# A two-layer decoder trunk on one core: modulation steps paced by matmul work, a packed rotary key, and a merge that takes its last head pair late

## The chip, the cores and the metric

The kernel runs on one core of a Trainium2 chip. The metric is the device time of one execution in microseconds (us). TensorE multiplies matrices into PSUM banks; VectorE, ScalarE and GpSimd do elementwise work; SyncE (SP) issues every DMA, in the order of its queue. Each engine runs its own instructions in order and waits on semaphores for what others produce.

## The reference

Two layers work on x, 1024 tokens by 1024 channels, in float32. Each layer is modulated by a vector `c`: shift, scale and gate vectors for two sub-layers come from one product with `w_ada`. The first sub-layer has one combined input projection, a stick-breaking attention, a latent attention (MLA) with rotary keys, and a gated merge. The second is an MLP with a squared ReLU.

```
mod = c_act @ w_ada[l] + b_ada[l]        # 6 vectors of 1024
shift1, scale1, gate1, shift2, scale2, gate2 = split(mod, 6)
h = rms_norm(x, g_mix_norm[l]) * (1 + scale1) + shift1
q_sb, k_sb, v_sb, q_lat, kv_lat, k_rope, gate_sb, gate_mla = split(h @ w_in[l])
o_sb  = stick_breaking(q_sb, k_sb, v_sb) @ w_sb_out[l]
q, kv = rms_norm(q_lat) @ w_q_up[l], rms_norm(kv_lat) @ w_kv_up[l]
k_pe  = rope(k_rope)                     # 32 channels, shared by 8 heads
o_mla = softmax_attention(q with rope, kv, k_pe) @ w_mla_out[l]
merged = sigmoid(gate_sb) * o_sb + sigmoid(gate_mla) * o_mla
x = x + gate1 * (merged @ w_mix_out[l])
h = rms_norm(x, g_mlp_norm[l]) * (1 + scale2) + shift2
x = x + gate2 * (square(relu(h @ w_up[l])) @ w_down[l])
```

After both layers, one more RMS norm gives the output.

## The kernel before

**Precision and tiles.** Activations lie transposed, channels on 128 partitions and tokens in two halves of 512. To keep float32 accuracy each operand is split in a high and a low part, and a product is three matmuls per 128 channels (`mm3_k`): high by high, high by low, low by high. A 1024-channel product of 128 outputs and one half is 24 matmuls of 512 columns into one bank.

**The planner.** The kernel is not emitted as it is written. `Plan.record` collects every operation with its tiles, `Plan.schedule` places them on five modelled engines by estimated costs, and `emit` writes them out in that order. TensorE's operations are due in the order in which they are recorded, and of those that are ready the earliest is taken; the due times of all others follow backwards from the TensorE work that needs them. Tiles of a class (`Cls`) take its slots strictly in the order of recording, and a slot that two classes share goes to the later class once the earlier has placed all its tiles. So where in the program a step is recorded decides how urgent it is.

**The modulation.** `modulation(l, parts)` is a generator. It makes a 1024-long vector in four pieces of 256: four steps per piece, each with one load of 256 KB of `w_ada` into a buffer of class `AD` and two products on VectorE (`mac`) into an accumulator of class `A`. `finish` then splits the accumulator (ScalarE copy, GpSimd subtraction, two more `A` tiles) and sums it over the partitions with four small matmuls into a `tp` bank. In the mixing sub-layer it makes parts 2 to 5 of the layer's own vectors, 64 steps. In the MLP it makes parts 0 and 1 of the next layer, 32 steps. `AD` has two buffers and `A` three. `finish` goes one step further at each load of the next piece, so a piece's first matmul is recorded two steps after its last load.

**The mixing sub-layer** (`layer`). First the latents (five jobs of `linear`, names `lraw`, `lh`, `ll`), then their norm (`lat_norm`), then a list of jobs: the rotary key (`kr_job`: 32 of the 128 weight columns in use), the first pair's queries, keys and values, and four gates. Here each half of a job takes two modulation steps. Then comes the loop over four head pairs with the products from the latents (weights in `qp` and `parts`), the rotary queries for every second pair, and a gate. Here each half takes one step, or two for a gate. Results are split and stored to DRAM by `keep_split` and `rope`, whose tiles come from `ltmp`: class `lt` in the first part, class `lt2`, four slots, in the loop.

**Attention and merge.** Attention works through pairs of heads, with other jobs filled in between. Its results go to DRAM by way of class `O`. Afterwards `outputs("mla")` loads them back through the six buffers of class `T`, splits them into `H` tiles, and `w_mla_out` is applied by `linear`, eight jobs of two halves, with `merge` as evacuation.

Of the kernel before, what the change touches and what calls it, by code (L numbers as in the profile page):

```python
# [20 lines left out]
P = 128  # L21
# [20 lines left out]
ON_ACT = (0, 2, 4, 6)  # L42

CHUNKS = (2, 2, 4)


def bc(ap):
# [128 lines left out]
class Plan:  # L176
    def __init__(self, nc):
        self.nc = nc
        self.ops, self.tiles = [], []
        self.slot_users = {}  # L180
        self.early = 0.0
        self.after = set()
        for n in ENG:
            setattr(self, n, Engine(self, n))

# [5 lines left out]
    def record(self, engine, method, a, k):  # L191
        a = tuple(View(x) if isinstance(x, PTile) else x for x in a)
        k = {n: View(x) if isinstance(x, PTile) else x for n, x in k.items()}
        outs, ins = [], []
        for i, x in enumerate(a):
            if isinstance(x, View):
                (outs if i == 0 and "out" not in k else ins).append(x)
        for n, x in k.items():
            if isinstance(x, View):
                (outs if n in ("out", "accum_out") else ins).append(x)  # L200
        op = Op()
        op.i = len(self.ops)
        op.eng = ENG[engine]
        if method == "dma_start":
            op.eng = "DMA"
        op.early = self.early
        op.func = str(k.get("func", "")).split(".")[-1]
        op.dur = cost(op.eng, method, a, k, outs, ins)
        op.succs, op.news, op.tiles = [], [], []
        nc = self.nc  # L210

        def fn():
            r = lambda x: x.resolve() if isinstance(x, View) else x
            getattr(getattr(nc, engine), method)(*[r(x) for x in a], **{n: r(x) for n, x in k.items()})  # L214
        op.fn = fn
        preds = set(self.after)
        for v in outs + ins:
            if getattr(v.tile.cls, "psum", False):
                v.box = [(0, n) for n in v.tile.shape]
        for v in ins:  # L220
            t = v.tile
            for box, o in t.writes:
                if overlap(box, v.box):
                    preds.add(o)
        for v in outs:
            t = v.tile
            for box, o in t.writes:
                if overlap(box, v.box):
                    preds.add(o)
            for box, o in t.reads:  # L230
                if overlap(box, v.box):
                    preds.add(o)
        for v in ins:
            v.tile.reads.append((v.box, op.i))
        for v in outs:
            t = v.tile
            t.writes = [(b, o) for b, o in t.writes if not covers(v.box, b)] + [(v.box, op.i)]
            t.reads = [(b, o) for b, o in t.reads if not covers(v.box, b) or o == op.i]
        preds.discard(op.i)
        op.preds = preds  # L240
        seen = set()
        for v in outs + ins:
            t = v.tile
            if id(t) in seen:
                continue
            seen.add(id(t))
            op.tiles.append(t)
            if not t.ops and t.cls.slots:
                op.news.append(t)
                t.cls.tiles.append(t)  # L250
            t.ops.append(op.i)
        self.ops.append(op)
# [237 lines left out]
class Trunk:  # L490
    def __init__(self, ctx, tc, I, out):
# [15 lines left out]
        slots = [f"s{i}" for i in range(46)]  # L507
        self.hs, self.ws, self.V = slots[:16], slots[16:22], slots[22:]
        self.T = self.cls("T", [f"t{i}" for i in range(6)])
        self.AD = self.cls("AD", ["ad0", "ad1"])  # L510
        self.A = self.cls("A", ["a0", "a1", "a2"])
        self.O = self.cls("O", ["o0", "o1"])
        self.ST = self.cls("ST", ["st0", "st1", "st2", "st3"])
        self.B = {}
        self.make_ps = maker(ps)
# [16 lines left out]

    def weight_slots(self, *more):
        self.W = {"raw": self.cls("raw", self.ws[:2]), "parts": self.cls("parts", self.ws[2:] + [*more])}

    def vcls(self, name, *idx):
        return self.cls(name, [self.V[i] for i in idx])
# [135 lines left out]
    def modulation(self, l, parts):  # L673
# [22 lines left out]
        for m in parts:  # L696
            for c0 in range(0, D, 256):
                acc = self.tile(self.A, [P, 256])
                for k0 in range(0, KT, 2):
                    w = self.tile(self.AD, [P, 2, 256])  # L700
                    v = I["w_ada"][l, k0 * P : (k0 + 2) * P, m * D + c0 : m * D + c0 + 256]
                    nc.sync.dma_start(out=w, in_=cols(v))
                    next(before, None)
                    for k in range(2):
                        self.mac(acc, w[:, k, :], k0 + k)
                    yield
# [421 lines left out]
    def layer(self, l, xT, ssq, before):  # L1128
# [3 lines left out]

        self.new_h()
        hh, hl = self.hh, self.hl

        qd, kd, vd, md, gd, od = {}, {}, {}, {}, {}, {}

# [50 lines left out]
        kr = 2176  # L1188

        def kr_w():  # L1190
            raw = self.tile(self.W["raw"], [P, KT, P])
            nc.gpsimd.memset(raw, 0.0)
            for i in range(2):
                nc.sync.dma_start(out=raw[:, :, 64 * i : 64 * i + 16], in_=win(kr + 16 * i, 16))
            return self.split_w(raw, KT)

        def lat_norm(b, tiles, width, g):
            for hf, sl in enumerate(HALVES):
# [20 lines left out]
        c_ll = self.vcls("ll", *range(5))  # L1219
        latl = [self.full(c_ll, F32R) for i in range(5)]  # L1220
        c_lt = self.vcls("lt", 15, 16, 17, 23, *range(5, 8))
        x_d = [self.dt([P, S]) for k in range(KT)]
        for k in range(KT):
            nc.sync.dma_start(out=x_d[k], in_=xT[k])
        if l == 0:
            for (_, evac, _), ps in zip(jobs, banks):
                evac(ps, HALVES[0])
            for (_, evac, _), w in zip(jobs, ws):
                ps = self.bank("pp")
                self.mm3(ps, w, hh, hl, HALVES[1], KT)  # L1230
                evac(ps, HALVES[1])
        self.weight_slots()
        if l > 0:
            for _ in self.linear(jobs[:4], hh, hl, KT, halves_first=True):
                pass
        for _ in self.linear(jobs[4:], hh, hl, KT):
            pass
        if l == 0:
            self.rope_tables(ltmp)
        cos, sin = self.full(c_cs), self.full(c_cs)  # L1240
# [1 line left out]
        nc.sync.dma_start(out=sin, in_=self.sin_d)  # L1242
        lat_norm(0, range(0, 3), QR, "g_q_lat")
        lat_norm(1, range(3, 5), KVR, "g_kv_lat")
        kr_job = (kr_w, lambda ps, sl: rope(ps, sl, 16, kpe_d), P)
        ada = self.modulation(l, [2, 3, 4, 5])
        for _ in self.linear([kr_job] + qkv(0) + [gate(m) for m in range(4)], hh, hl, KT):
            next(ada, None)
            next(ada, None)

        c_qp, c_lt = self.vcls("qp", 16, 17, *range(18, 24)), self.vcls("lt2", 15, 5, 6, 7)

        def by_heads(src, k0, k1, c0, nh, width, groups, cls):

# [24 lines left out]
        for p in range(4):  # L1279
# [2 lines left out]
                wq = q_parts(p // 2)  # L1282
            q_w = part(wq, p % 2 * P)
            for _ in self.linear([(q_w, self.keep_split(mq[p], ltmp), P)], lath, latl, 3):
                next(ada, None)
            wkv = kv_parts(p)
            k_w, v_w = part(wkv, 0), part(wkv, P)
            kv_jobs = [(k_w, self.keep_split(mk[p], ltmp), P), (v_w, self.keep(mv[p]), P)]
            for _ in self.linear(kv_jobs, lath[3:], latl[3:], 2):
                next(ada, None)  # L1290
            if p % 2 == 0:
                g = p // 2
                qr_d[g] = self.two()
# [1 line left out]
                for sl in HALVES:  # L1295
                    ps = self.bank("pp")
                    self.mm3(ps, w, lath, latl, sl, 3)
                    rope(ps, sl, 64, qr_d[g])
                    next(ada, None)
            for _ in self.linear([gate(4 + p)], hh, hl, KT):  # L1300
                next(ada, None)
                next(ada, None)
        for _ in ada:
            pass

        self.attention_banks()

        def sb_head(p, e):
            def load():
# [103 lines left out]
            return evac  # L1413

        oh, ol = outputs("mla")
        for _ in self.linear([(out_w(I["w_mla_out"], m), merge(m), P) for m in range(KT)], oh, ol, 4):
            pass
        for k in range(KT):
            nc.sync.dma_start(out=xT[k], in_=x_d[k])
# [17 lines left out]
        for _ in range(KT):  # L1437
            next(steps)

        V, hs = self.V, self.hs  # L1440
        c_f, c_b1 = self.cls("hf", hs[:8]), self.cls("b1", hs[8:])
        c_b12, c_b22 = self.cls("b12", V[8:12]), self.cls("b22", V[12:16])
        c_t13, c_t24 = self.cls("t13", V[16:]), self.cls("t24", V[:8])
# [18 lines left out]

        NP = DFF // P // 2
        hid = [self.dt([P, 8, HALF]) for m in range(NP)]
        ada = self.modulation(l + 1, range(2)) if l + 1 < DEPTH else iter(())

        def hidden(f):
# [258 lines left out]
```

## Time and profile before

| | |
|---|---|
| median of 3 runs | 3226.88 us (3220.65 to 3230.88) |
| the profiled execution's own time | 3225.95 us |
| its span, first to last instruction | 3224.2 us |
| TensorE (PE) matmul busy | 3081.9 us, 96% |
| VectorE (DVE) busy | 2219.3 us, 69% |
| ScalarE (ACT) busy | 1537.2 us, 48% |
| GpSimd (POOL) busy | 1177.9 us, 37% |
| moved by DMA | 527.20 MB, mean 164 GB/s |

PE is the matmul row, and weight loads (PEld) overlap it. Matmul records overlap in a pipeline, so the time of one is read from start to start. PEclk is the granted clock as a share of full speed. DMA share is the mean busy share of the core's 16 DMA engines. Nearly all operations are recorded by one helper line, L214, so operations are told apart by their tiles, written out<-in.

### The profile page before, as it was taken

To read this page: it belongs to the slowest core of one execution; us is meant where nothing else is said; L and a number is where in the kernel's file an instruction comes from. 1 tells how busy PE (TensorE), PEld (TensorE's weight loads), DVE (VectorE), ACT (ScalarE), POOL (GpSimd) and SP (SyncE) were. 2 spreads that over 40 slices of the span, in tenths; PEclk is the share of its full clock that TensorE was granted. 3 is DMA by queue.
4 is the path that set the end of the run, shared out by engine and by line. 5 is a ranking of instruction groups with operands and counts; after the bars stand their busy time and mean duration, and the time that the engine had idled before them with its cause. 6 is when DMAs were issued, how large, how long until landed. Compare 5 with 4: busy or idle time off the path is not lost. (4 is left out here: it accounts for less than half of the span.)

```text
span 3224.2 us, 42816 instructions
## 1 busy us (share of the span) xinstructions
PE 3081.9 (96%) x14823; PEld 2500.9 (78%) x14823; DVE 2219.3 (69%) x3238; ACT 1537.2 (48%) x2633; POOL 1177.9 (37%) x942
## 2 busy tenths in 40 slices
PE   5998999999999999999999989999999999999998
PEld 4876777888777787877777767878887777888786
DVE  7476656668667676698867546656766777559886
ACT  4432556667344444434443235666754444444343
POOL 3222434211233654345432324441113345534442
PEclk9999999999999999999999999999999999999999
DMA  6458645445843654955144774454466445476522
GB/s 223 152 175 260 189 119 130 106 110 156 288 129 112 204 185 167 286 158 173 66 133 128 248 223 126 114 148 107 115 212 200 134 138 179 157 227 212 182 85 86
DMA packets 439868, 527.20 MB, mean 164 GB/s; under 512 B 32338, under 2 KB 310500, under 8 KB 439652
## 3 DMA queue, kind: packets, MB, share of 16 engines
q1 hardware_dynamic: 439652, 524.48, 53.1%
q8 instruction: 117, 1.92, 0.3%
q14 instruction: 99, 0.81, 0.1%
HBM read 362.36 MB, written 162.00 MB: 163 GB/s over the span
## 5 line engine op out<-in xcount | busy, mean ns | idle before, releaser
L214 PE MATMUL pp<-H,parts 128*128 128x512 f32 x4032 | 1062.5, 407 | 9.2 <-ACT H L214 8.1
L214 PEld LDWEIGHTS pp<-H,parts 128*128 128x128 f32 x4032 | 739.8, 191 | 158.9 <-ACT H L214 9.3
L214 PE MATMUL pp<-bo,ws 128*128 128x512 f32 x2688 | 628.4, 395 | 14.0 <-POOL ws L214 7.5
L214 PEld LDWEIGHTS pp<-bo,ws 128*128 128x128 f32 x2688 | 503.2, 188 | 136.8 <-POOL ws L214 10.1
L214 POOL TENSOR_TENSOR parts<-raw,parts 128x1024 fp32r<-128x1024 f32 (+2 forms) x158 | 321.1, 2033 | 707.4 <-ACT parts L214 663.2
L214 POOL TENSOR_TENSOR ws<-wr,ws 128x1024 fp32r<-128x1024 f32 x112 | 299.8, 2684 | 370.0 <-ACT ws L214 344.7
L214 PE MATMUL pp<-t,pw 128*128 128x512 f32 x1344 | 324.3, 400 | 12.4 <-ACT pw L214 7.6
L214 PEld LDWEIGHTS pp<-t,pw 128*128 128x128 f32 x1344 | 255.2, 191 | 75.2 <-ACT pw L214 9.4
L214 ACT CAST parts<-raw 128x1024 fp32r<-128x1024 f32 (+2 forms) x158 | 141.6, 897 | 258.5 <-PE pp L214 231.9
L214 DVE TENSOR_TENSOR wtl<-tp,wth 128x512 fp32r<-128x512 f32 (+3 forms) x384 | 207.5, 551 | 67.8 <-ACT wth L214 65.6
L214 PE MATMUL pp<-b,pw 128*128 128x512 f32 x1008 | 243.1, 398 | 0.4 <-DVE u L214 0.3
L214 DVE SCALAR_TENSOR_TENSOR x<-pp,const,x 128x512 f32<-128x512 f32 x256 | 180.6, 742 | 89.0 <-PE pp L214 88.9
L214 DVE TENSOR_TENSOR_SCAN F<-F,sc 128x128 f32<-128x128 f32 (+7 forms) x128 | 171.7, 1349 | 94.2 <-ACT F L214 72.5
L214 DVE SCALAR_TENSOR_TENSOR A<-AD,const,A 128x256 f32<-128x256 f32 x280 | 182.9, 653 | 75.9 <-DMA AD<-in_w_ada 70.8
L214 DVE TENSOR_TENSOR bo<-T,bo 128x512 fp32r<-128x512 f32 x224 | 221.6, 1038 | 17.7 <-ACT bo L214 17.2
L214 ACT CAST wth<-tp 128x512 fp32r<-128x512 f32 (+3 forms) x384 | 180.8, 481 | 92.8 <-PE tp L214 87.3
L214 POOL TENSOR_TENSOR pw<-T,pw 128x512 fp32r<-128x512 f32 x112 | 161.1, 1457 | 173.9 <-ACT pw L214 166.3
L214 PEld LDWEIGHTS pp<-b,pw 128*128 128x128 f32 x1008 | 189.2, 189 | 45.3 <-DVE u L214 0.8
L214 POOL TENSOR_TENSOR W<-W,F 128x127 f32<-128x127 f32 (+7 forms) x128 | 153.5, 1205 | 188.1 <-ACT W L214 103.3
L214 ACT CAST bo<-T 128x512 fp32r<-128x512 f32 x224 | 135.1, 620 | 175.2 <-DMA T<-dram 133.9
L214 ACT CAST ws<-wr 128x1024 fp32r<-128x1024 f32 x112 | 116.8, 1049 | 157.0 <-PE pp L214 138.6
L214 PE MATMUL tp<-const,W 128*128 128x128 f32 x1152 | 183.1, 273 | 5.0 <-DVE wtl L214 4.4
(153 smaller groups left out, 4581.1 us busy)
## 6 DMA issues: line engine op xcount, KB each, us to landing
T<-dram SPq DMA_DIRECT2D x352, 256.0 KB
dram<-T SPq DMA_DIRECT2D x208, 256.0 KB
dram<-u SPq DMA_DIRECT2D x92, 512.0 KB
AD<-in_w_ada SPq DMA_DIRECT2D x160, 256.0 KB
raw<-in_w_in SPq DMA_DIRECT2D x68, 512.0 KB
wr<-in_w_down SPq DMA_DIRECT2D x64, 512.0 KB
pr<-in_w_up SPq DMA_DIRECT2D x56, 512.0 KB
sq<-dram SPq DMA_DIRECT2D x96, 256.0 KB
```

The costliest lines, as they stand in the source:

```text
L214: getattr(getattr(nc, engine), method)(*[r(x) for x in a], **{n: r(x) for n, x in k.items()})
```

## The change

- `Plan` sums the modelled cost of all TensorE operations in `pe`. From the latents on, `pace` takes as many modulation steps as `pe` has grown since then in units of 3.0 us (`ADA_STEP`). The fixed counts per job are gone.
- `finish` is advanced once at the first load of the next piece (the split), and its matmuls are recorded after that piece's last load.
- In the mixing sub-layer `AD` has a third buffer, the slot `V[7]`. That slot was `lt2`'s fourth. `A` has five slots; two are those of `O`, which is now made anew for the attention.
- The rotary key packs high and low weights into the 128 columns, in blocks of 32. Each half takes 16 matmuls, and the blocks are added after a copy out of the bank.
- The first two jobs of the MLA output projection take three head pairs for both halves in four banks first, and then the last pair for all four.

```
+ADA_STEP = 3.0
 Plan.__init__:
+        self.pe = 0.0
 Plan.record:
+        if op.eng == "PE":
+            self.pe += op.dur
 Trunk.__init__:
-        self.AD = self.cls("AD", ["ad0", "ad1"])
-        self.A = self.cls("A", ["a0", "a1", "a2"])
-        self.O = self.cls("O", ["o0", "o1"])
+    def mod_slots(self, *more):
+        self.AD = self.cls("AD", ["ad0", "ad1", *more])
+        self.A = self.cls("A", ["a0", "a1", "a2", "o0", "o1"])
 modulation:
                     nc.sync.dma_start(out=w, in_=cols(v))
-                    next(before, None)
+                    if k0 == 0:
+                        next(before, None)
 layer:
         def kr_w():
-            raw = self.tile(self.W["raw"], [P, KT, P])
+            raw = self.tile(self.W["raw"], [P, KT, 2, 32])
             nc.gpsimd.memset(raw, 0.0)
             for i in range(2):
-                nc.sync.dma_start(out=raw[:, :, 64 * i : 64 * i + 16], in_=win(kr + 16 * i, 16))
-            return self.split_w(raw, KT)
+                nc.sync.dma_start(out=raw[:, :, i, :16], in_=win(kr + 16 * i, 16))
+            w = self.tile(self.W["parts"], [P, KT, 2, 2, 32], F32R)
+            nc.scalar.copy(out=w[:, :, :, 0], in_=raw)
+            nc.gpsimd.tensor_sub(w[:, :, :, 1], raw, bc(w[:, :, :, 0]))
+            return w
+
+        def kr_products():
+            w = kr_w()
+            for sl in HALVES:
+                ps = self.bank("pp")
+                for k in range(KT):
+                    a = w[:, k].rearrange("p a b c -> p (a b c)")
+                    nc.tensor.matmul(ps, a, hh[k][:, sl], start=k == 0, stop=False)
+                    nc.tensor.matmul(ps, a, hl[k][:, sl], start=False, stop=k == KT - 1)
+                s, u = ltmp(), ltmp()
+                nc.scalar.copy(out=s, in_=ps)
+                for r in (0, 64):
+                    nc.scalar.copy(out=u[r : r + 32], in_=ps[r + 32 : r + 64])
+                    nc.vector.tensor_add(s[r : r + 32], s[r : r + 32], u[r : r + 32])
+                rope(s, sl, 16, kpe_d)
+                yield
...
+        self.mod_slots(V[7])
+        ada = self.modulation(l, [2, 3, 4, 5])
+        begin, taken = nc.pe, 0
+        def pace():
+            nonlocal taken
+            while nc.pe - begin > taken * ADA_STEP:
+                next(ada, None)
+                taken += 1
...
         (latents: pace() after every half)
-        kr_job = (kr_w, lambda ps, sl: rope(ps, sl, 16, kpe_d), P)
-        ada = self.modulation(l, [2, 3, 4, 5])
-        for _ in self.linear([kr_job] + qkv(0) + [gate(m) for m in range(4)], hh, hl, KT):
-            next(ada, None)
-            next(ada, None)
-        c_qp, c_lt = self.vcls("qp", 16, 17, *range(18, 24)), self.vcls("lt2", 15, 5, 6, 7)
+        first = self.linear(qkv(0) + [gate(m) for m in range(4)], hh, hl, KT)
+        for _ in self.chain([kr_products(), first]):
+            pace()
+        c_qp, c_lt = self.vcls("qp", 16, 17, *range(18, 24)), self.vcls("lt2", 15, 5, 6)
...
         (loop over the pairs: pace() in place of each next(ada, None))
         self.attention_banks()
+        self.O = self.cls("O", ["o0", "o1"])
...
-        for _ in self.linear([(out_w(I["w_mla_out"], m), merge(m), P) for m in range(KT)], oh, ol, 4):
+        first = [(out_w(I["w_mla_out"], m)(), merge(m)) for m in range(2)]
+        first = [(w, evac, sl, self.bank("pp")) for w, evac in first for sl in HALVES]
+        for w, evac, sl, ps in first:
+            for k in range(3):
+                self.mm3_k(ps, w, oh, ol, sl, k, 4)
+        for w, evac, sl, ps in first:
+            self.mm3_k(ps, w, oh, ol, sl, 3, 4)
+            evac(ps, sl)
+        for _ in self.linear([(out_w(I["w_mla_out"], m), merge(m), P) for m in range(2, KT)], oh, ol, 4):
             pass
...
         (MLP)
+        self.mod_slots()
         ada = self.modulation(l + 1, range(2)) if l + 1 < DEPTH else iter(())
```

## Rows read from the trace of the kernel before

**Rows 1.** Waits of TensorE, whole trace: who waited for whom, total us, times, longest.
```profile
PE tp L214 <- ACT A L214: 30.9, 20, 3.1
```

**Rows 2.** Waits of TensorE from 120 to 340 us.
```profile
PE tp L214 <- ACT A L214: 19.3, 10, 3.1
```

**Rows 3.** Waits of TensorE from 1660 to 1930 us.
```profile
PE tp L214 <- ACT A L214: 11.6, 10, 2.6
```

**Rows 4.** Waits of TensorE from 900 to 1660 us.
```profile
PE tp L214 <- POOL A L214: 4.5, 1, 4.5
```

**Rows 5.** Slices of layer 0: us, PE busy (matmuls), granted clock, DMA share, GB/s.
```profile
190.00:200.00 10.00, 7.10 (x27) 0.83 0.48 142
...
270.00:280.00 10.00, 8.62 (x34) 0.83 0.88 283
280.00:320.00 40.00, 37.19 (x164) 1.00 0.88 275
...
330.00:340.00 10.00, 6.83 (x29) 0.91 0.96 249
```

**Rows 6.** Layer 1: PE, PEld, DVE, ACT, POOL busy, clock, DMA share, GB/s.
```profile
1860.00:1870.00 10.00, 9.85 (x38) 8.07 (x39) 4.68 (x10) 3.20 (x8) 1.10 (x2) 0.83 0.93 306
...
1890.00:1900.00 10.00, 7.36 (x30) 5.66 (x29) 5.67 (x11) 2.65 (x5) 2.75 (x7) 0.90 0.73 220
```

**Rows 7.** Tile AD, 150 to 350 us: ns min/median/max, first to last; VectorE idle until.
```profile
L214 DVE SCALAR_TENSOR_TENSOR A<-AD,const,A x98: 460/485/2586, 183.6 to 347.9; 128x256 f32<-128x256 f32 x98
L214 SPq DMA_DIRECT2D AD<-in_w_ada x54: 367/383/1002, 184.1 to 343.8; - x54
...
  DMA AD<-in_w_ada: 38.9, 25
```

**Rows 8.** Tile AD, 1725 to 1905 us.
```profile
L214 SPq DMA_DIRECT2D AD<-in_w_ada x54: 367/383/902, 1739.3 to 1891.4; - x54
```

**Rows 9.** TensorE in order of time, layer 1's latents: start, us, operation, count.
```profile
1654.79 53.37 PE L214 MATMUL pp<-H,parts 128*128 128x512 f32 x229
```

**Rows 10.** Layer 0, 160 to 200 us; columns as in rows 6.
```profile
160.00:180.00 20.00, 20.00 (x90) 16.26 (x89) 19.89 (x33) 14.68 (x23) 4.04 (x2) 1.00 0.25 76
180.00:200.00 20.00, 17.10 (x72) 13.60 (x71) 19.45 (x30) 6.88 (x15) 10.22 (x10) 0.91 0.48 144
```

**Rows 11.** VectorE in order of time: the last piece of the latent norm.
```profile
190.26 0.68 DVE L214 TENSOR_TENSOR ll<-lraw,lh 128x512 fp32r<-128x512 f32 x1
```

**Rows 12.** TensorE in order of time: the first matmul from the normed latents.
```profile
217.28 0.39 PE L214 MATMUL pp<-lh,qp 128*128 128x512 f32 x1
```

**Rows 13.** ScalarE, first head pair of layer 0; in brackets the idle time before.
```profile
219.91 0.59 ACT L214 CAST lt<-pp 128x512 fp32r<-128x512 f32 x1 [1.11 <-PE pp L214]
221.99 0.59 ACT L214 CAST lt<-pp 128x512 fp32r<-128x512 f32 x1 [1.49 <-PE pp L214]
225.84 0.59 ACT L214 CAST lt<-pp 128x512 fp32r<-128x512 f32 x1 [3.26 <-DVE A L214]
...
232.28 0.59 ACT L214 CAST lt<-pp 128x512 fp32r<-128x512 f32 x1 [1.70 <-DMA dram<-lt]
```

**Rows 14.** TensorE where layer 0's MLA output projection begins.
```profile
838.91 0.49 PE L214 MATMUL pp<-H,parts 128*128 128x512 f32 x1 [2.73 <-ACT H L214]
```

**Rows 15.** Tile O, 780 to 860 us: the attention's last stores.
```profile
L214 SPq DMA_DIRECT2D dram<-O x6: 451/452/452, 783.7 to 810.6; - x6
```

**Rows 16.** ScalarE in order of time: the last operand of that projection.
```profile
845.55 0.62 ACT L214 CAST H<-T 128x512 fp32r<-128x512 f32 x1 [1.63 <-DMA T<-dram]
```

**Rows 17.** VectorE, first head pair of layer 0.
```profile
221.51 0.68 DVE L214 TENSOR_TENSOR lt<-pp,lt 128x512 fp32r<-128x512 f32 x1
...
226.72 0.69 DVE L214 TENSOR_TENSOR lt<-pp,lt 128x512 fp32r<-128x512 f32 x1 [0.94 <-DMA dram<-lt]
```

**Rows 18.** SP's queue, first head pair of layer 0: start, us, DMA, count.
```profile
223.63 2.55 SPq L214 DMA_DIRECT2D AD<-in_w_ada  x2
226.22 2.46 SPq L214 DMA_DIRECT2D dram<-lt  x4
```

More of the change, by code (lines that the diff above doesn't have):

```diff
@@ L1134, in layer @@
         hh, hl = self.hh, self.hl
+        V = self.V
         qd, kd, vd, md, gd, od = {}, {}, {}, {}, {}, {}
@@ L1234, in layer @@
             for _ in self.linear(jobs[:4], hh, hl, KT, halves_first=True):
-                pass
+                pace()
         for _ in self.linear(jobs[4:], hh, hl, KT):
-            pass
+            pace()
         if l == 0:
@@ L1244, in layer @@
         lat_norm(1, range(3, 5), KVR, "g_kv_lat")
-        kr_job = (kr_w, lambda ps, sl: rope(ps, sl, 16, kpe_d), P)
-        ada = self.modulation(l, [2, 3, 4, 5])
-        for _ in self.linear([kr_job] + qkv(0) + [gate(m) for m in range(4)], hh, hl, KT):
-            next(ada, None)
-            next(ada, None)
-        c_qp, c_lt = self.vcls("qp", 16, 17, *range(18, 24)), self.vcls("lt2", 15, 5, 6, 7)
+        first = self.linear(qkv(0) + [gate(m) for m in range(4)], hh, hl, KT)
+        for _ in self.chain([kr_products(), first]):
+            pace()
+        c_qp, c_lt = self.vcls("qp", 16, 17, *range(18, 24)), self.vcls("lt2", 15, 5, 6)
         def by_heads(src, k0, k1, c0, nh, width, groups, cls):
@@ L1284, in layer @@
             for _ in self.linear([(q_w, self.keep_split(mq[p], ltmp), P)], lath, latl, 3):
-                next(ada, None)
+                pace()
             wkv = kv_parts(p)
@@ L1289, in layer @@
             for _ in self.linear(kv_jobs, lath[3:], latl[3:], 2):
-                next(ada, None)
+                pace()
             if p % 2 == 0:
@@ L1298, in layer @@
                     rope(ps, sl, 64, qr_d[g])
-                    next(ada, None)
+                    pace()
             for _ in self.linear([gate(4 + p)], hh, hl, KT):
-                next(ada, None)
-                next(ada, None)
+                pace()
         for _ in ada:
@@ L1438, in layer @@
             next(steps)
-        V, hs = self.V, self.hs
+        hs = self.hs
         c_f, c_b1 = self.cls("hf", hs[:8]), self.cls("b1", hs[8:])
```

## The prediction

> **What bounds the kernel now.** I read four views in this order: where TensorE waited in the whole trace, then in the two stretches where a layer's modulation vectors are made, then those stretches slice by slice, then the loads and the vector steps that feed them. TensorE is busy for 96% of the span, so only what it waits for, and the matmuls it need not do, can give time back. Its waits for the modulation's split (`tp <- ACT A`) come to 30.9 us [rows 1], 19.3 of them in layer 0 [rows 2] and 11.6 in layer 1 [rows 3]; one more wait for the same vectors stands in the MLP, 4.5 us [rows 4]. Behind such stalls the granted clock falls from its upper level (2.4 GHz) to the lower (1.2) for a part of a slice. A granted clock of 0.83 over 10 us is 1.7 us of work not done, so layer 0's slices lose (0.17 + 0.17 + 0.09) x 10 = 4.3 us [rows 5] and layer 1's (0.17 + 0.10) x 10 = 2.7 us [rows 6]: 7.0 us that hang on the same stalls.
>
> Why do the splits come late? In layer 0, 54 modulation loads are issued between 184.1 and 343.8 us, one in 2.96 us; in layer 1, 54 in 152.1 us, one in 2.82 [rows 7, 8]. A 512-column matmul takes 53.37/229 = 0.233 us [rows 9]. The code asks for two steps (one load each) per 24 matmuls up to the heads' loop, one in 2.80 us, and in that loop for 12 steps per 108 matmuls, one in 2.10 us. The chain of load, two products and buffer release gives one in 2.8 to 3.0. It falls behind, VectorE sits 38.9 us waiting for the loads [rows 7], and TensorE, which meets a piece's first matmul two steps after its last load, waits.
>
> **Pace, lag, slots.** A step per 3.0 us of the planner's matmul cost (0.2163 us each by its formula) is one per 13.9 matmuls, 3.23 us on the chip. That is slower than the 2.82 to 2.96 that the old chain reached with two buffers and a short lead. The matmuls of a piece now come four steps later, and five A slots instead of three let two pieces wait ready: the lead grows from about two steps to more than six, some 20 us, against a longest stall of 3.1 us. So nearly all of the 30.9 us should go. I leave 3 us for the last piece of each layer, which still drains without lag: -28 (bounds -31 and -15, the last if half of the stalls stay), with it 0.9 of the clock loss, -6 (bounds -7 and 0). The lag holds for the MLP's modulation too: -4 of the 4.5 us (0 to -4.5).
>
> What pays for the earlier steps: their loads now go through SP's queue and the DMA engines from the latents on, where the engines are 0.25 to 0.48 busy (160 to 200 us, [rows 10]) against 0.88 in the later slices [rows 5]. The extra slots also let up to four more loads (1 MB, 3.8 us at the 275 GB/s of [rows 5]) slip into layer 0's start. On VectorE the stretch from 160 to 200 is full: 39.3 of 40 us [rows 10]. It gets some six more steps, each two products of 0.485 us [rows 7], so 6 us, and from the rotary key below 2.7 us. What is late then is the latent norm, whose last pieces end near 191 us [rows 11], and whose first reader on TensorE starts at 217.3 [rows 12]: 26 us of cover, some 20 after TensorE's own gain by then. So I put 2 us on all this (0 to 8).
>
> **Rotary key.** 24 matmuls per half become 16; two halves, two layers: 32 x 0.233 = 7.5 us off TensorE, in a stretch where it has no gap [rows 10]. The new evacuation adds, per half, three ScalarE copies (nearest: 0.59 us from a bank [rows 13]) and two 32-partition additions on VectorE (nearest: 0.68, [rows 11]), 2.7 us of VectorE a layer, counted above; ScalarE is busy 14.7 and 6.9 of 20 us there [rows 10]. The bank comes free after one copy rather than after VectorE's rotary products. -7.5, 0 if another engine took over there.
>
> **Merge.** TensorE waits 2.73 us when the attention output projection begins [rows 14], once a layer. The change puts 36 matmuls ahead of the last head pair's. But the last attention store is issued at 810.6 us [rows 15], 28 us before that stall, and the last cast of an operand (845.55, [rows 16]) comes 7 us after it without a wait of its own. What is late are the first operands, which queue for the six T buffers behind the stores of the other branch; that the change doesn't touch. Behind it, the third weight tile waits until two of four banks are done: its ScalarE and VectorE work was covered by 15 matmuls and is now covered by six. -1 (bounds -5.5, both stalls gone, and +3).
>
> **The buffer that is taken away.** The third load buffer was the fourth slot of `lt2`, which holds the split results of queries and keys until their stores land, and the rotary working tiles. This has a price. In the first pair the splits go in at 219.91, 221.51 and 221.99; with four slots, the fifth, sixth and seventh start at 225.84, 226.72 and 232.28 [rows 13, 17], the last two on a store. So slots are held 5.9, 5.2 and 10.3 us. Part of the longest is the SP queue: its store is issued at 226.22, behind two modulation loads that took 2.55 us [rows 18]. Two pairs of heads hold 20 stored tiles and 4 short ones (about 3 us each), while TensorE needs 198 x 0.233 = 46 us for them. With holding time L, four slots need (20 L + 12)/4 us, three need (20 L + 12)/3: 44 us at L = 6, 51 at L = 7. Four slots are never short at these values; three are at the edge. The third load buffer takes the 2.55 us off SP, so I take L = 6, where only bursts cost: 2 us for each two pairs, four times: +8. Below, 0 if L falls to 5 (37 us). Above, at L = 7.4 it is 53 us, 7 over, +28.
>
> The Trainium skill's page "DMA: Bandwidth & Descriptors" (section Anatomy of one DMA) gives about 2.0 us fixed plus bytes/436 GB/s for a transfer. By that a 256 KB store lands in an estimated 2.6 us, a slot is free after some 4 us, and the sum would be 8 us lower. The trace disagrees for this stretch: the store issued at 226.22 freed its slot 6.1 us later [rows 13, 18].
>
> **Sum.** -28 - 6 - 4 - 7.5 - 1 + 8 + 2 = -36.5 us. The profiled execution took 3225.95 us (1.75 outside its span), 0.93 under the median of the runs. 3225.95 - 36.5 = 3189.5; against the median, 3190 us.
>
> **Rivals.**
> *A: the smaller slot pool takes over (slower).* Evacuations stand in line for stores, banks fill, TensorE waits for `pp`. For: slots were held up to 10.3 us. Against: TensorE had no such wait in either stretch [rows 2, 3], and the loads that block SP thin out. Without the slot term the sum is -44.5. At L = 9 two pairs need 64 us, 18 over, four times 72: 3225.95 - 44.5 + 72 = 3253. It turns slower by more than 0.3% from L = 8.4 on (60 us, 14 over, 56). Chance 0.08.
> *B: the loop stays bound by transfers.* DMA engines at 0.88 and 275 GB/s [rows 5] have little left, so loads stay late at any pace and two thirds of the stalls remain: -10 - 2 for stalls and clock, -7.5, and nothing else of note: 3226 - 19.5 = 3206. Against: by the pace 512/13.9 = 37 of a layer's 64 loads lie ahead of the heads' loop, where before it was 10 + 33.2/2.96 = 21 (ten ahead of 184.1 us, the rest at the old rate to 217.3). Chance 0.10.
> *C: VectorE is the new bound before the heads' loop.* The products and the rotary key's additions stand in a stretch that is full already. Some products take 2.586 us instead of 0.485 [rows 7]. If ten of the sixteen added operations lost those 2.1 us, VectorE would be 9 + 21 us later, 10 past its cover, in each layer: 3189.5 + 20 = 3210. It begins from five on. The skill's page "SBUF — State Buffer" (section SBUF: two separate sides) has it that VectorE operations with two SBUF inputs and GpSimd operations that read SBUF exclude each other for a whole instruction; the long products fit that rule, and it speaks against moving work there. Chance 0.04.
> *D: the planner doesn't do what the code says.* It orders by its own costs, so the pace only moves due times, and every later instruction order may shift with it: the gain is the 7.5 us of matmuls plus or minus the listed waits elsewhere: 3219. Chance 0.06.
>
> **Chances and range.** The forecast has 0.72 (its own range 3168 to 3212), A 0.08, B 0.10, C 0.04, D 0.06. Best ends together (-31 - 7 - 4.5 - 7.5 - 5.5) give 3170; upwards the range goes on to B, C and most of D. 80%: 3166 to 3221. A measurement tells about 0.3% (9.7 us) from no change. Faster by more: the forecast, B, most of C, a part of D: 0.84. Within: 0.09. Slower: A, 0.07.
>
> **What would show it.** Right: the `tp <- ACT A` waits fall from 30.9 to under 5 us; slices at 0.83 clock vanish from both stretches; modulation loads begin in the latents and end before the attention; the rotary key has 32 matmuls a layer; the merge's stall stays near 2.7 us. The slot term shows as new `pp` waits on `lt` in the heads' loop, 8 us in all, and longer idle of ScalarE and VectorE until `dram <- lt`. Wrong: more than 28 us of such waits (A), modulation waits above 15 us with full DMA slices (B), a wait of the first `lh` matmuls (C), or losses in the attention or the MLP, which I cost at nothing.

## The result, and the profile after

The changed kernel takes 3213.28 us in the median (20 executions, 3206.58 to 3226.48) against 3231.17 before (20, 3220.65 to 3238.16): ratio 0.9948, 95% interval 0.9939 to 0.9957. It is 17 us faster by the ratio, as forecast in sign, and less than half of the 36.5 us in size. The profile was taken on the slowest of the 20 executions (3226.48 us). So a second profile of the same kernel stands beside it below, from an execution of 3209.42 us; its six executions gave a ratio of 0.9938 (0.992 to 0.9956).

TensorE's waits in the changed kernel, whole trace (`ws` are the weights of the MLP's down projection, `u` the MLP's combinations, `vT` the attention's values, `lt` the split results of queries and keys):

```profile
PE pp L218 <- POOL ws L218: 12.6, 10, 2.4
PE pp L218 <- ACT u L218: 11.2, 3, 9.2
...
PE tp L218 <- DMA vT<-dram: 10.1, 7, 2.2
PE tp L218 <- ACT A L218: 8.2, 7, 2.1
...
PE pp L218 <- DVE T L218: 5.9, 3, 3.4
PE pp L218 <- DVE lt L218: 5.6, 3, 2.7
...
PE pp L218 <- ACT lt L218: 1.2, 1, 1.2
```

The same in its second profile:

```profile
PE pp L218 <- ACT u L218: 11.0, 3, 9.2
...
PE pp L218 <- POOL ws L218: 10.1, 8, 2.4
PE tp L218 <- DMA vT<-dram: 8.3, 7, 1.9
PE tp L218 <- ACT A L218: 7.3, 4, 2.1
```

The kernel before, in the rows of the same view that answer to these:

```profile
PE pp L214 <- POOL ws L214: 7.5, 6, 1.7
...
PE tp L214 <- DMA vT<-dram: 5.4, 4, 2.5
...
PE pp L214 <- ACT u L214: 4.8, 3, 2.7
```

What was to go has gone: the waits for the modulation's split fell from 30.9 us [rows 1] to 8.2 and 7.3 us (under 5 was forecast), all of it in layer 0, and the one in the MLP [rows 4] is gone. But all rows of this view together come to 132.7 us before and 136.0 and 124.8 after. `ACT u` and `ws` in the MLP and `vT` in the attention have grown, `lt` in the heads' loop is new. The first profile is of an execution as long as the profiled one of before (3225.95 us), so its sum can't show a gain. The second is 16.5 us shorter, with 7.9 us less of waits and 8.1 us less of matmuls. The mean granted clock is 0.988 before and 0.986 and 0.988 after: the clock gave nothing.

Where the second profile gains and loses shows in the same work: first and last matmul of each layer's stick-breaking scores (`sc<-sq`), and of layer 0's down projection (`bo,ws`). Before:

```profile
L214 PE MATMUL sc<-sq,sq x192: 274/390/793, 331.1 to 582.6; 128*128 128x512 f32 x96, 128*128 128x256 f32 x64, 128*128 128x384 f32 x32
L214 PE MATMUL pp<-bo,ws x1344: 387/394/505, 1321.2 to 1645.7; 128*128 128x512 f32 x192
L214 PE MATMUL sc<-sq,sq x192: 275/390/502, 1913.5 to 2163.4; 128*128 128x512 f32 x96, 128*128 128x256 f32 x64, 128*128 128x384 f32 x32
```

The changed kernel's second profile:

```profile
L218 PE MATMUL sc<-sq,sq x192: 274/391/776, 320.6 to 573.8; 128*128 128x512 f32 x96, 128*128 128x256 f32 x64, 128*128 128x384 f32 x32
L218 PE MATMUL pp<-bo,ws x1344: 387/395/793, 1312.9 to 1643.8; 128*128 128x512 f32 x192
L218 PE MATMUL sc<-sq,sq x192: 275/389/506, 1898.3 to 2147.8; 128*128 128x512 f32 x96, 128*128 128x256 f32 x64, 128*128 128x384 f32 x32
```

Up to layer 0's attention it gains 10.5 us, and from the end of the down projection to layer 1's attention 13.3. In the down projection it loses 6.4, from layer 0's attention to that projection 2.2, and behind layer 1's start of attention it gains 1.4: 16.6 us in all (spans of 3224.2 and 3207.6).

### The profile page after: what moved, and what is told of

It reads as the page before. It is cut to its first block, busy times and chain, and to the rows that moved or that the text cites. A ratio compares the mean times of both kernels' runs of the same rounds, so it can differ in the third digit from the quotient of the medians.

```text
span 3224.7 us, 42818 instructions
## 1 busy us (share of the span) xinstructions
PE 3079.3 (95%) x14791; PEld 2497.0 (77%) x14791; DVE 2242.2 (70%) x3246; ACT 1542.2 (48%) x2647; POOL 1184.0 (37%) x942
## 4 chain that ended last, share of the span: by engine, by line
PE 60%; DVE 16%; DMA 12%; issue 5%; ACT 5%; POOL 1%; SPq 1%; DVEq 0%; ACTq 0%; POOLq 0%
PE pp L218 47%; PE tp L218 8%; PE sc L218 4%; DVE A L218 3%; DMA T<-dram 3%; DVE bo L218 2%; DMA dram<-T 2%; DVE T L218 2%; DMA AD<-in_w_ada 2%; DVE x L218 1%; DVE wr L218 1%; DMA dram<-lt 1%; ACT F L218 1%; ACT W L218 1%; DVE F L218 1%
## 5 line engine op out<-in xcount | busy, mean ns | idle before, releaser
L218 PE MATMUL pp<-bo,ws 128*128 128x512 f32 x2688 | 635.3, 397 | 19.0 <-POOL ws L218 12.6
L218 DVE TENSOR_TENSOR bo<-T,bo 128x512 fp32r<-128x512 f32 x224 | 218.5, 1022 | 17.1 <-ACT bo L218 16.6
L218 DVE SCALAR_TENSOR_TENSOR A<-AD,const,A 128x256 f32<-128x256 f32 x280 | 196.6, 702 | 45.6 <-DMA AD<-in_w_ada 40.4
L218 PE MATMUL pp<-merged,parts 128*128 128x512 f32 x768 | 182.0, 398 | 5.8 <-POOL parts L218 2.9
```

## The experiments

All ratios are against the kernel before on the same chip; TensorE times are from one profile each. "The changed kernel" is the one under study.

### The parts alone

**The changed kernel again.** No edit.

> The changed kernel, unaltered, once more with a profile. Its first profile (3226.48 us) was the slowest of its 20 executions, so it says little of where the median's gain sits. If the loss in the attention and the MLP seen there (up to the first layer's attention it is 8.5 us ahead, at the end 0) belongs to the order of the instructions, this profile shows the same new waits (ws, u, vT) at the same places. If it belongs to that execution, they are gone and the lead is kept to the end: about 3213 us, ratio 0.995.

3209.42 us, ratio 0.9938 (0.992 to 0.9956). It reaches layer 0's attention at 320.6 us (331.1 before) and keeps more of the lead, but the waits for `u`, `ws` and `vT` stand at the same places. They belong to the order of the instructions; how long each is belongs to the execution. Not all of it is the modulation's: with the rotary key alone (below) `vT` is 8.4 us and `ws` 8.5.

**The modulation alone.** The diff without `kr_products` and without the merge's new order:

```
-        for _ in self.chain([kr_products(), first]):
+        kr_job = (kr_w, lambda ps, sl: rope(ps, sl, 16, kpe_d), P)
+        for _ in self.linear([kr_job] + qkv(0) + [gate(m) for m in range(4)], hh, hl, KT):
...
-            for k in range(3):
-                self.mm3_k(ps, w, oh, ol, sl, k, 4)
...
+        for _ in self.linear([(out_w(I["w_mla_out"], m), merge(m), P) for m in range(KT)], oh, ol, 4):
```

> The modulation part alone (pace, lag, third load buffer, five A slots); rotary key and merge as before. By the prediction's terms -28 - 6 - 4 + 8 + 2 = -28 us, ratio 0.991. If the modulation gives less than predicted because other waits take its place in the same stretch, about -10 to -15 us (0.996). If the planner's new order elsewhere takes it back, anything from -10 to +5 us with the modulation waits gone all the same.

Ratio 0.9963 (0.9947 to 0.998): 12 us faster, between 6 and 17. The split's waits fall to 4.2 us, yet all waits together only from 132.7 to 129.8: `ACT u` is 10.4, `vT` 10.0, `ws` 9.6, `lt` 8.8. That profile is of an execution of 3226.42 us, no shorter than the one of before, so its sum of waits doesn't show where the 12 us of the median lie.

**The rotary key alone.** `kr_products` in place of `kr_job`; the slots, the lag and the steps as before:

```
-                    if k0 == 0:
-                        next(before, None)
+                    next(before, None)
...
-                pace()
+                next(ada, None)
```

> The rotary key in 32 matmuls alone, all else as before. By the count of matmuls -7.5 us, ratio 0.9977. If that stretch isn't bound by TensorE (VectorE full, modulation loads late), the time saved there is spent waiting for the modulation: 0 to -2 us. If the new order elsewhere counts for more than the part, it lies outside -10 to 0.

Ratio 0.9978 (0.9966 to 0.9989), 7 us faster (4 to 11), which agrees with the price of 32 matmuls.

**The merge alone.** The kernel before with the changed kernel's lines ahead of `self.linear` in the merge (`for k in range(3)`, then the fourth pair and `evac`) and nothing else of the diff.

> The merge that takes the last pair late, alone. Predicted -1 us (between -5.5 and +3), with the wait of about 2.7 us in each layer still there. If the last pair was what came late, -4 to -5.5 us and that wait gone. Outside this range: the planner's order elsewhere.

Ratio 1.0005 (0.9992 to 1.0018). From 828 to 1000 us the waits for `H` and weights get shorter by as much as the next product's wait for `merged` is new:

```profile
PE pp L214 <- DVE merged L214: 2.7, 1, 2.7
PE pp L214 <- ACT H L214: 1.8, 1, 1.8
PE pp L214 <- POOL parts L214: 1.2, 3, 0.6
```

Before, in the same stretch:

```profile
PE pp L214 <- POOL parts L214: 2.8, 2, 1.6
PE pp L214 <- ACT H L214: 2.7, 1, 2.7
```

The three parts add up: -12 - 7 + 1.6 = -17 us. What is missing is missing in the modulation, as far as single ratios tell (see the control).

### Layer 0: can the steps be early?

**Sums in another bank.** `sums` is "pp" in the mixing sub-layer and "tp" in the MLP.

```
-            ps = self.bank("tp")
+            ps = self.bank(sums)
```

> The changed kernel, but the modulation's sums in the mixing sub-layer go to a bank of pp instead of tp. Theory: in layer 0 the modulation stands still from 130 to 187 us (no product on VectorE), since its tp bank is recorded behind the four tp banks of the latent norm and banks are given in the order of recording; the steps that were to be early are made up later at more than the chain can do, and four waits of 7.3 us with their clock loss remain. Then here the products go on through 130 to 187 us, the waits for ACT A in layer 0 fall from 7.3 to under 3 us, and the time falls by 5 to 12 us against the changed kernel (3198 to 3206 us, ratio to before near 0.991). Rival: the loads or VectorE (busy 9.8 of 10 us from 160 to 190) hold it back there in any case: same time within 4 us, products still missing, or the latent norm late instead.

Ratio 0.9982 (0.9971 to 0.9994), slower than the changed kernel. The view is VectorE's time in the modulation's products by stretches (us, busy, count, clock, DMA share, GB/s). The changed kernel's second profile:

```profile
90.00:130.00 40.00, 10.30 (x16) 1.00 0.52 170
130.00:180.00 50.00, 0.00 (x0) 1.00 0.50 159
180.00:310.00 130.00, 56.45 (x96) 0.96 0.77 251
```

With the sums in pp:

```profile
130.00:180.00 50.00, 10.15 (x22) 0.90 0.67 208
```

The hold-up is real and the bank order is its cause: the products now run through. But the first matmul from the normed latents comes at 224.8 us (213.1 in the changed kernel's second profile), and layer 0's attention at 332.0 (320.6). Up to there TensorE now waits for banks of pp, above all until VectorE has added a sum (`const`) and so freed its bank. With the sums in pp, from 120 to 226 us:

```profile
PE pp L218 <- DVE const L218: 3.9, 2, 3.6
PE pp L218 <- ACT T L218: 1.4, 1, 1.4
```

All waits of that view come to 6.9 us; in the second profile up to its first matmul from the normed latents they are 2.0. All engines from 160 to 190 us, in the changed kernel's second profile:

```profile
160.00:190.00 30.00, 30.00 (x138) 24.58 (x137) 29.61 (x47) 23.60 (x35) 10.63 (x7) 1.00 0.25 84
```

With the sums in pp:

```profile
160.00:190.00 30.00, 28.21 (x116) 22.27 (x116) 26.54 (x45) 16.71 (x25) 6.02 (x4) 0.94 0.56 174
```

VectorE is busy for 29.61 of 30 us there without one product, but for only 26.54 with eight of them. So that a full VectorE is what delays the rest isn't shown. The trace shows the sums taking banks from the latents' products: of the 11.7 us of delay, 4.9 are longer waits, and a granted clock of 0.90 in place of 1.00 from 130 to 180 us is an estimated 5. What the freed steps would be worth with a bank of their own stays open.

**Steps from the rotary key on**, with `ADA_STEP = 2.45`.

```
-            while nc.pe - begin > taken * ADA_STEP:
+            while going and nc.pe - begin > taken * ADA_STEP:
...
+        ada = self.modulation(l, [2, 3, 4, 5])
+        begin, taken, going = nc.pe, 0, True
```

> The changed kernel with the steps starting at the rotary key, as before, and 2.45 us of modelled cost to a step instead of 3.0, so that they end in the loop over the pairs; slots, lag, buffer and the rest as changed. If starting with the latents is worth little, since the latent norm's banks hold the steps up in layer 0 anyway, layer 0 reaches its attention at the same time (320 to 323 us), and the total is within 4 us. If the early start is what took the waits away, they come back: ACT A over 12 us, 5 to 12 us slower.

Ratio 0.9978 (0.9966 to 0.999); attention of layer 0 at 326.9 us. The split's waits came to 6.6 us, and 2.3 for GpSimd: slots, third buffer and pace take most of them away without the early start. Layer 0's attention begins 6 us later than in the second profile, but the step sizes below alone put it between 320.6 and 326.8, so what the early start is worth isn't shown.

### Lag, slots, buffer

**No lag.**

```
-                    if k0 == 0:
-                        next(before, None)
+                    next(before, None)
```

> The changed kernel without the lag: the split advances at every load again, in both sub-layers. If the lag is what took the waits for ACT A from 30.9 to 7.3 us, they come back to 15 or more and the time rises by 8 to 15 us. If pace and slots did it, the time stays within 4 us. The burst in the MLP should stay, since the slots do.

Ratio 0.9954 (0.994 to 0.9969), the split's waits 4.6 us: the lag does nothing that shows.

**Two load buffers, four `lt2` slots.**

```
-        self.mod_slots(V[7])
+        self.mod_slots()
-        ..., self.vcls("lt2", 15, 5, 6)
+        ..., self.vcls("lt2", 15, 5, 6, 7)
```

> The changed kernel with two load buffers and lt2's fourth slot back. The prediction put 8 us on the missing slot; the waits of pp for lt came to 6.8 us in one profile and 2.5 in the other. If the slot costs that, these waits are gone and the time falls by 3 to 8 us. If the third load buffer is worth more than the slot, the waits for ACT A grow by more than that and the time rises by up to 8 us. If neither, within 3 us.

**Third buffer and four `lt2` slots.**

```
-        c_qp, c_lt = self.vcls("qp", 16, 17, *range(18, 24)), self.vcls("lt2", 15, 5, 6)
+        c_qp, c_lt = self.vcls("qp", 16, 17, *range(18, 23)), self.vcls("lt2", 15, 5, 6, 23)
```

> The changed kernel with the third load buffer and four slots in lt2 too; the eighth slot of the query weights (qp) is given up for it, whose next group is due only two head pairs later. This prices the missing slot with all else kept. By the prediction's term the waits of pp for lt (2.5 to 6.8 us in all) vanish and the time falls by up to 8 us. If those waits belong to the SP queue rather than to the slots, they stay and the time is the same within 3 us.

Without the third buffer the ratio is 0.9993 (0.9979 to 1.0008), with both 0.996 (0.9939 to 0.9981). TensorE's waits with two buffers and four slots:

```profile
PE tp L218 <- ACT A L218: 15.1, 12, 3.5
...
PE pp L218 <- DVE lt L218: 9.5, 5, 3.4
```

With the third buffer and four slots:

```profile
PE pp L218 <- DVE lt L218: 10.3, 4, 5.0
...
PE tp L218 <- ACT A L218: 4.9, 5, 2.0
```

Four slots don't take the `lt` waits away: 10.3 us against 1.3 and 5.6 with three. So the slot count isn't their cause. The third load buffer is worth having: the split's waits go from 15.1 to 4.9 us.

**Four A slots.**

```
-        self.A = self.cls("A", ["a0", "a1", "a2", "o0", "o1"])
+        self.A = self.cls("A", ["a0", "a1", "a2", "o0"])
```

> The changed kernel with four A slots instead of five. Theory: the fifth lets a third piece of the next layer's modulation be made ahead of time, 24 products between 1440 and 1510 us instead of 16 to 17, in a stretch of the MLP's second half where VectorE has no room (19.5 us of products where there were 9), and that stretch is 6 us longer in every kernel with the new modulation. With four slots only two pieces fit: 16 products, the stretch back to some 325 us from 331, time 3 to 6 us lower than the changed kernel. Rival: fewer slots mean later splits in the mixing sub-layer; the waits for ACT A grow and eat it: same within 3 us, or slower. If the stretch stays at 331 with 16 products, the products aren't its cause.

Ratio 0.9987 (0.9972 to 1.0002). In the MLP's second half it did what was expected (below), but `vT` and the split wait longer (14.8 and 10.5 us). That these eat the gain is argued, not shown: `vT` is 15.5 us with five slots and 3.1 us to a step, too.

### The MLP and the stretch before layer 1

**The MLP's modulation as before.**

```
-        self.mod_slots()
+        self.mod_slots(mixing=False)
```

`mixing=False` gives three A slots and advances the split at every load.

> The changed kernel with the MLP's modulation as it was: three A slots and the split advanced at every load. Theory: five slots let two pieces run in one burst (25 products between 1040 and 1120 us where before there were 8), just where VectorE makes the MLP's combinations, and TensorE waits 9.2 us for ACT u and loses clock. Then that wait falls to under 2 us, the wait for POOL A of some 4.5 us is back, and the time falls by 5 to 10 us. Rival: the wait belongs to the whole new order and stays: within 3 us of the changed kernel.

Ratio 0.997 (0.9955 to 0.9985). `ACT u` falls to 3.2 us and the 4.5 us for `POOL A` are back; the MLP's loop takes 296.3 us, as before the change (296.4), against 294.8 and 295.7. The theory had the time falling by 5 to 10 us against the changed kernel; it didn't fall. The wait hangs on the fifth slot: it is 4.3 us with four A slots, and 10.9 without the lag. In the changed kernel's second profile it is this one:

```profile
1083.67 5.49 PE L218 MATMUL pp<-t,pw 128*128 128x512 f32 x12 [9.20 <-ACT u L218]
```

Modulation products on VectorE from 1020 to 1120 us, before:

```profile
1020.00:1120.00 100.00, 8.71 (x9) 0.97 0.52 172
```

The changed kernel's second profile:

```profile
1020.00:1120.00 100.00, 27.95 (x32) 0.91 0.58 194
```

**A gate.** In layer 1 no modulation step may start before the first matmul of the latents; with 3.0 and with 3.1 us to a step.

```
-        begin, taken = nc.pe, 0
+        begin, taken, op0 = nc.pe, 0, len(nc.ops)
...
+            if l > 0:
+                nc.after = {next(o.i for o in nc.ops[op0:] if o.eng == "PE")}
             while nc.pe - begin > taken * ADA_STEP:
                 next(ada, None)
                 taken += 1
+            nc.after = set()
```

> The changed kernel, but in layer 1 no step of the mixing modulation may begin before the first matmul of the latents. Theory: the 24 products made ahead between 1400 and 1520 us take 4 to 5 us of TensorE's time through late VectorE and GpSimd work (waits for ws 7.6 to 8.5 us instead of 4.4). Then here no such product stands there, TensorE is busy 317 to 319 us of the stretch from 1330 to 1660 (changed kernel 313 to 315), and the time falls by about 4 us, unless layer 1's steps, which lose their lead, wait again for ACT A. Rival: the stretch loses its 4 to 5 us without these products too.

> The same with 3.1 us to a step. If the products ahead of time are the cause and not a chance order, the stretch from 1330 to 1660 us is again at 317 to 319 us of matmuls, and the kernel is 3 to 5 us faster than the ungated one of 3.1 (3227). If not, the same as that one within 3 us.

Ratios 0.993 (0.9904 to 0.9956) and 0.9957 (0.9941 to 0.9973), against 0.9938 to 0.9948 and 0.9981 (below) without the gate. First TensorE's busy time from 1330 to 1660 us, then the modulation's products from 1400 to 1520 us. Before:

```profile
1330.00:1660.00 330.00, 318.12 (x1359) 1.00 0.51 162
1400.00:1520.00 120.00, 8.97 (x16) 1.00 0.56 170
```

Changed, second profile:

```profile
1330.00:1660.00 330.00, 314.72 (x1327) 0.99 0.49 160
1400.00:1520.00 120.00, 21.46 (x24) 0.97 0.57 175
```

Four A slots:

```profile
1330.00:1660.00 330.00, 317.46 (x1340) 0.99 0.51 165
1400.00:1520.00 120.00, 11.66 (x16) 0.97 0.57 176
```

Gated:

```profile
1330.00:1660.00 330.00, 316.83 (x1351) 1.00 0.48 154
1400.00:1520.00 120.00, 0.00 (x0) 1.00 0.50 155
```

Gated, 3.1 us (without the gate 314.58):

```profile
1330.00:1660.00 330.00, 319.26 (x1348) 0.98 0.48 155
```

Products that are made ahead of time there cost TensorE some 4 us of this window. All twenty profiles agree, those told below too: the eleven with 24 products have 311.1 to 316.1 us of matmuls in that stretch (mean 314.3), one with 20 has 313.8, the eight with 16 or none 316.8 to 320.6 (mean 318.6). The window is fixed in time, so it doesn't hold the same work in each. The down projection from its first to its last matmul does. Gated; 3.1 us without the gate; gated, 3.1 us:

```profile
L218 PE MATMUL pp<-bo,ws x1344: 387/394/507, 1314.8 to 1641.1; 128*128 128x512 f32 x192
L218 PE MATMUL pp<-bo,ws x1344: 387/394/796, 1322.0 to 1656.5; 128*128 128x512 f32 x192
L218 PE MATMUL pp<-bo,ws x1344: 387/394/796, 1318.0 to 1644.9; 128*128 128x512 f32 x192
```

With the gate it takes 326.3 in place of 330.9 and 334.3 us, and at 3.1 us to a step 326.9 in place of 334.5: 5 to 8 us less. In the eleven profiles with 24 products it takes 330.1 to 337.1 us, in the eight with 16 or none 322.4 to 328.7. Layer 1 loses nothing by the gate: from there to its attention it takes 254.8 us, against 254.5 in the second profile. In time the gate is worth 3 to 8 us by these ratios, of one sign at both step sizes, but no more than the control below leaves open.

**Later steps in the MLP**, and **the MLP as before**, each on top of the gate. The second's edit is `mod_slots(mixing=False)`, as above. The first's, at all three places of the MLP's loop:

```
-            next(ada, None)
+            if m > 4:
+                next(ada, None)
```

> The gated kernel, with the MLP's modulation steps beginning at the fifth of its pairs of 128 rows (m = 5) instead of the second; all 32 steps still fit in the loop. Theory: the burst after the first pieces falls where VectorE makes the first combinations and costs TensorE 9 us of waiting (ACT u). Moved behind them, that wait falls under 3 us, the MLP's loop takes 287 to 291 us instead of 294.5, and the time is 4 to 8 us lower than the gated kernel's 3204. Rival: the burst costs as much wherever it falls: within 3 us.

> The gated kernel with the MLP's modulation as before the change (three A slots, the split advanced at every load). The wait for ACT u goes and the one for POOL A (4.5 us) comes back; without the gate this was even in the MLP's loop (296.3 against 294.8 to 295.7 us). So within 4 us of the gated kernel.

Ratios 0.9905 (0.9886 to 0.9924), at 3199.23 us the fastest of all, and 0.9941 (0.9918 to 0.9965). But the theory behind the first fell: the products still stand in one burst (32 from 1020 to 1120 us) and `ACT u` still takes 8.9 us at once. The planner makes the first pieces as early as buffers allow, wherever they are recorded. Why that kernel is faster than the gated one is open; other stretches differ by a few microseconds, no more than between step sizes.

### The control: the step size

**3.1, 2.9 and 2.8 us to a step** instead of 3.0.

> A control: the changed kernel with 3.1 us to a step instead of 3.0. No theory here sees more than 2 us in it. What it differs by is what a new order of the instructions does on its own, and the bound below which the differences of the other kernels say nothing.

> A second control: 2.9 us to a step. If 3.0 was a lucky order and 3.1 a usual one, this lies near 3220 to 3228; if 3.1 was the odd one, near 3213.

> A third control: 2.8 us to a step. As for 2.9: with four step sizes the mean and the spread of the modulation part can be told from one order's luck. Usual: 3215 to 3228.

Ratios 0.9981 (0.9967 to 0.9996), 0.9964 (0.9951 to 0.9977) and 0.9947 (0.993 to 0.9964), with 0.9948 and 0.9938 for 3.0. No reason of mine sees more than 2 us in such a step, and they are up to 14 us apart. The planner orders every instruction anew, and that alone is worth several microseconds. The mean of the four sizes is 0.9959, 13 us faster than before: 7 of it the rotary key, some 6 the modulation. The changed kernel's further 4 us may be its order's chance. Differences under some 10 us between two kernels of these, by time alone, say nothing of their edits; the stretches of the traces do.

## Why the prediction was right or wrong

**Which step failed.** "What pays for the earlier steps", 2 us for VectorE and the transfers, together with losses in the attention and the MLP, which the text "cost at nothing" without giving a reason. In their place the down projection alone lost 6.4 us to products made ahead of time (5 to 8 by the gate). Two gains were too large besides: the clock's -6 came to nothing, and the MLP's -4 to about -1.

The waits named did fall, by 23 to 27 of 30.9 us and the 4.5 us in the MLP, but others came. By the stages above: up to the two attentions -28 - 6 - 7.5 + 8 + 2 = -31.5 us were forecast and -23.8 measured, in the down projection 0 and +6.4, everywhere else -5 and +0.8. These are single profiles, and step sizes alone move a stage by a few microseconds; the loss in the down projection is the one that the gate confirms. The modulation alone gave 12 us where its terms make 28.

- *Layer 0.* I gave the latent norm 20 us of cover and saw no obstacle. The code of before had one: four `tp` banks of the norm stand ahead of the sums in the order of recording. From 130 to 180 us no product was made; afterwards 96 were made in 130 us, one load in 2.7 us, about the old chain's pace, and 7 to 8 us of waits stayed. By the code the third load buffer isn't there yet either: `V[7]` is also a slot of `lt`, which gives it up only once the first part's tiles are all placed. With the sums in pp the products ran, and TensorE waited 6.9 us, nearly all for banks. Rival C had the place right; that VectorE is the bound there isn't shown.
- *The MLP (-4).* The wait of 4.5 us went, one of 9.2 us came with the fifth A slot, which lets two pieces run in one burst where VectorE makes the combinations. The loop is 0.7 to 1.6 us shorter, in place of 4.
- *The MLP's second half.* Not in my text: the slots let a third piece of layer 1's vectors be made ahead there. The gate, at two step sizes, takes 5 to 8 us off that stretch, and four A slots 2 to 6; what of it reaches the end isn't settled.
- *The clock (-6).* Nothing. The stalls that cost clock were replaced by others: from 250 to 260 us the second profile has a granted clock of 0.67, from 1080 to 1100 one of 0.76.

**The lag** has no part in it that shows, against what I wrote: without it the waits are as short. Of the other parts the third load buffer shows (15.1 to 4.9 us of the split's waits).

**The slot (+8).** New waits of `pp` for `lt` came: 2.5 to 6.8 us in all, near the size. But a fourth slot doesn't remove them, so the reason, slots held by stores, isn't shown; what makes them is open. The transfer time that the text cites from the Trainium skill's page "DMA: Bandwidth & Descriptors" (section Anatomy of one DMA) is given there for transfers issued by GpSimd; here SyncE issues them all. The sum didn't use it.

**Right.** The rotary key: -7.5 forecast, -7 measured, and 32 matmuls fewer, though the control leaves open how much of the 7 us is their price. The merge: -1 forecast, none measured, and the wait stayed at the first operands (1.8 of 2.7 us) as said. Rivals A and B: the `lt` waits stayed far under 28 us, and the split's waits went although the transfers were as busy as before. Rival D was too narrow: the planner did what the code says, but its new order is worth as much as a part of the change.

## What to carry to other kernels

Work that is moved earlier has a price where it lands: look up the stretch in which each load and product will stand, which engine is full there, and which banks or buffers are given out in order ahead of it. Where slots are added, ask what will now be made ahead of time, and gate it if that stretch has no room: here a stretch of matmuls got 5 to 8 us longer by products made ahead of time. Before a part is judged by time in a planned kernel, change a number that shouldn't matter and see how far that moves it.

## What the runs showed that I had not expected

Waits that were taken off TensorE came back for the greater part as others: 132.7 us in all before and 124.8 in the changed kernel's second profile, although the modulation's own fell by 28 us. One kernel's 20 executions lie 20 us apart, so that a single profile can hide a gain of 17. And the modulation's products don't cost the same everywhere. From 840 to 1400 us the 64 for the MLP take 51.2 us before and 52.2 in the changed kernel's second profile, 0.80 and 0.81 us each, bunched or not. The ones for layer 1 behind them, up to 1520 us, take 8.97 us for 16 before, 0.56 each, and 21.46 us for 24, 0.89 each. It isn't their number: with the rotary key alone 16 take 14.11 us, 0.88 each. What makes them dearer there is open.
